# Fewer dense expert blocks, ranked by more heads, and more gathered rows, in a one-core decoder step

## The chip, the cores and the metric

The kernel runs on one core of a Trainium2 chip. The metric is the time of one execution on the device in microseconds. The kernel before took 3285.18 us (median of three runs, 3284.6 to 3286.1).

## The reference, cut to what matters

One layer of a decoder trunk is computed for 512 prompt tokens and 64 sample tokens of width 2048: modulated norm, an input projection, a recurrent and a convolutional head group, an output projection, and then PEER, an expert layer that takes most of the time. Everything is float32.

```python
q = (xb @ w_q).reshape(PEER_BLOCK, PEER_HEADS, 2, HALF_DIM)          # 8 heads
sc = jnp.einsum('thpk,pnk->thpn', q, sub_keys)                       # 2 x 128 keys
v1, i1 = lax.top_k(sc[:, :, 0], 16); v2, i2 = lax.top_k(sc[:, :, 1], 16)
cand = v1[..., :, None] + v2[..., None, :]
cidx = i1[..., :, None] * N_KEYS + i2[..., None, :]
top, pos = lax.top_k(cand, 16)
eidx = jnp.take_along_axis(cidx, pos, axis=-1)                       # 16 of 16384 experts per head
g = jax.nn.softmax(top, axis=-1)
act = jax.nn.gelu(jnp.einsum('td,thkd->thk', xb, expert_u[eidx])) * g
return jnp.einsum('thk,thkd->td', act, expert_v[eidx])
```

A token thus has 8 x 16 = 128 picks among 16,384 experts. The 128 experts that share a first key `i1` are called a block here; there are 128 blocks.

## The kernel before

**Two ways to an expert.** The blocks are ranked by how often the prompt tokens choose their first key. The first `L` = 84 in rank are dense: every prompt token is multiplied with all 128 experts of such a block, and the products count with the gate weight, which is zero where the token did not pick the expert. Picks in the other 44 blocks, and all picks of the sample tokens, are gathered: an indirect DMA fetches one row of `u` or `v` (2,048 floats, 8,192 bytes) for each of 128 partitions, and VectorE multiplies it.

**Dense part.** A block's matrix is split into two float32r parts, `xhi` on ScalarE (line 904) and `xlo` on GpSimd (line 905), and a product takes three matmuls (hi x hi, hi x lo, lo x hi). The u products come first: `u_half` (line 1357) works on half a block at a time, 24 matmuls of 128x512, so 168 half blocks. They then leave `actd` in DRAM. The v products follow in steps of four blocks by a quarter of the width: `v_column` (line 1377) is called four times in a step with 12 matmuls each. `GROUPS` says over how many blocks a PSUM sum runs before VectorE adds it into `acc` (line 1399); the first group's sum is copied by ScalarE. There are M = 84 steps; the last nine are the tail, with the norm and the output beside them, and all gathered rows must be used by the step ahead of them (`last = M - VQ - ENDS`).

**Gate weights.** `g_pair`, `g_scale`, `g_mm` and `g_out` build, for eight tokens at a time, the weights of all dense blocks as a product of two one-hot matrices (line 1555) during the u products, and `g_out` writes them to DRAM, `gd`. For every four blocks (`sg`) `load_group` brings `actd` back as `actr`, `load_weights` brings the weights as `gsb` in four quarters on ScalarE's DMA queue, `weigh` multiplies them on VectorE (line 1320), and `halve` makes the two parts `ahi` (ScalarE) and `alo` (VectorE, line 1331) for the v products. The dictionary `jobs` says at which column of which step each of these is issued.

**Gathered part.** `count` counts each token's picks outside the dense blocks, `sort` orders the tokens by that count, and `SORTED` cuts the order into groups (first token, tokens, slots). A group of 128 tokens has a slot column for each pick; in a group of 64 each token has two partitions ("lanes"), so twice the picks. `slots` finds the picks by repeated top-8 (lines 1168 and 1170). Places without a pick get an index beyond the table, which moves nothing. `gather_u` first loads the group's tokens (`h2r`, then `hT` on ScalarE, line 1218), then fetches a row per slot (line 1203, issued by GpSimd) and takes the dot product (`dot`, line 1231); `gather_v` multiplies and adds into `accB` (line 1259) and at the end scatters the sum to `accd` with an indirect DMA (line 1270), a group's second lane by an accumulating one. The 64 sample slots come first. So there are 64 + 147 = 211 rows of u and as many of v. If a token has more picks than its slots, `flag` is set, and a branch at the end computes all picks of the groups exactly, 128 u and 128 v rows for each.

**Order.** All this is laid out by hand: from the last head's queries on, each engine runs its instructions in the order in which the program issues them. Inside a loop over half blocks, the generator `choice` (last head, softmax, count, sort), then `all_slots`, hand out pieces with a cost, and rows are issued by `RATE` until the slots are done, evenly after that. `EARLY_V` v rows are used during the u products, the rest in the v products, spread evenly over columns; up to four rows are fetched ahead there. `E0` is the half block from which the weights are all written and the first two `sg` are loaded. A block's number is read from `blk` by SyncE when its load is issued.

**Ranking.** `choose` adds, for the first `HEADS_COUNTED` = 4 heads, which keys are in a token's top 8 (`cnt`, line 754). `rank_keys` mixes these counts with a guess from the keys' norms and leaves `perm` and `blk`, before the last heads are computed.

Of the kernel before, what the change touches and what calls it, by code (L numbers as in the profile page):

```python
# [30 lines left out]
NA = NP  # L31
NG = T - NA
NE = 128
L = 84
SG = 4
GROUPS = (8,) * 10 + (4,)
# [5 lines left out]
SORTED = ((0, 64, 34), (64, 128, 43), (192, 128, 33), (320, 128, 27), (448, 64, 10))  # L42
# [6 lines left out]
RATE = (1.0, 1.7)  # L49
PIECE_G = 6.3  # L50
HEADS_COUNTED = 4
FULL_ROWS = 1.25
LAG = 3
PAIRS = 6
EARLY_V = 24
# [24 lines left out]
def build(ctx, tc, A, O, dbg=None):  # L80
# [598 lines left out]
    actp.tile([128, 24], F32, name="shift_l", bufs=1)  # L679
# [19 lines left out]
    gd = dr.tile([NCH, 128, L, TC], F32, name="gd")  # L699
# [46 lines left out]
    def choose(h, s, z):  # L746
# [6 lines left out]
        if h < HEADS_COUNTED and z != "S":  # L753
            V.scalar_tensor_tensor(cnt, s[:, 0:128], 0.5 * NEG, cnt, op0=ALU.is_lt, op1=ALU.add)
# [175 lines left out]

    def rank_keys():

        row = rt2.tile([128, 128], F32, name="rk_row")
        q = rt2.tile([128, 128], F32, name="rk_q")
        low = rt2.tile([128, 128], F32, name="rk_low")
        c = rt2.tile([128, 3], F32, name="rk_c")
# [13 lines left out]
        yield  # L950
        pk = pbank("g", "rk1", 2)
        PE.transpose(pk[:, 0:128], row, ident)
        V.tensor_copy(c[:, 0:1], pk[:, 0:1])
# [6 lines left out]
        PE.matmul(pk[:, 0:128], rowi.to_broadcast([128, 128]), low, start=True, stop=True)  # L960
        V.tensor_copy(perm, pk[:, 0:128])
        V.tensor_copy(blk, perm[0:1, :])
        yield

# [189 lines left out]
    def slots(i):  # L1154
# [19 lines left out]
        if n < 128:  # L1174
            V.tensor_copy(sl[n:, :, 0:c], sl[n:, :, c:2 * c])
# [65 lines left out]
    def gather_v(i):  # L1241
# [7 lines left out]
        def add(j):  # L1249
# [22 lines left out]
            for o in range(0, 128, n):  # L1272
                after.append([gu[0] + 2 + 4 * (o > 0), lambda o=o: out(o)])
# [6 lines left out]
    VO = (0, 2, 1, 3, 5, 4)  # L1280
# [179 lines left out]
    def choice():  # L1460
# [97 lines left out]
    def g_out(b, pg):  # L1558
# [15 lines left out]
    E0 = NU2 - 18  # L1574
# [24 lines left out]
    for n in range(NU2):  # L1599
# [61 lines left out]
        for sg, o, first in ((0, 1, 0), (1, 8, 1)):  # L1661
            if n - E0 == o + 1:
                load_group(sg)
            if 0 <= n - E0 - o + first < 4:
# [232 lines left out]
```

## Time and profile before

| | |
|---|---|
| median of the runs, us | 3285.18 (3284.6 to 3286.1) |
| profiled execution, us | 3270.15 |
| its span, us | 3268.2 |
| mean granted TensorE clock | 0.979 |
| TensorE, VectorE, ScalarE, GpSimd busy in the span | 95%, 66%, 33%, 53% |
| HBM read, written, MB | 865.21, 68.90 |
| first u product, first v product, us | 1198.9, 2263.0 |

The profile is one execution, read from the hardware's records. TensorE's busy time is modelled and its matmuls overlap, so how long a row of them took is read from the chain of work that ended last, where pieces stand with start and length. An engine's row in a table by stretches gives busy time with the number of instructions; "idle before" names what ended the wait. A DMA share of 1 means that the core's 16 DMA engines had packets in work all the time.

### The profile page before, as it was taken

To read this page: it belongs to the slowest core of one execution; us is meant where nothing else is said; L and a number is where in the kernel's file an instruction comes from. 1 tells how busy PE (TensorE), PEld (TensorE's weight loads), DVE (VectorE), ACT (ScalarE), POOL (GpSimd) and SP (SyncE) were. 2 spreads that over 40 slices of the span, in tenths; PEclk is the share of its full clock that TensorE was granted. 3 is DMA by queue.
4 is the path that set the end of the run, shared out by engine and by line. 5 is a ranking of instruction groups with operands and counts; after the bars stand their busy time and mean duration, and the time that the engine had idled before them with its cause. 6 is when DMAs were issued, how large, how long until landed. Compare 5 with 4: busy or idle time off the path is not lost.

```text
span 3268.2 us, 53659 instructions
## 1 busy us (share of the span) xinstructions
PE 3113.4 (95%) x20695; PEld 2636.8 (81%) x20695; DVE 2144.7 (66%) x3238; ACT 1074.2 (33%) x1672; POOL 1725.1 (53%) x985
## 2 busy tenths in 40 slices
PE   5999999999989999999989999998999999999997
PEld 2688889899979998887778888776788877788776
DVE  5455521243346898887988888856667787778745
ACT  3244311132232222222656666522322222222222
POOL 2233233344343336666656666656767676777642
PEclk8999999999989999999999999999999999999998
DMA  9834566624342228989879898999999988898964
GB/s 363 298 136 140 172 214 207 209 82 135 128 156 70 70 89 280 314 315 371 314 287 387 323 391 337 375 353 350 369 354 374 376 310 287 324 366 323 353 189 146
DMA packets 305109, 869.09 MB, mean 266 GB/s; under 512 B 37610, under 2 KB 81514, under 8 KB 256650
## 3 DMA queue, kind: packets, MB, share of 16 engines
q1 hardware_dynamic: 165216, 390.87, 34.6%
q0 software_dynamic: 62880, 386.64, 30.2%
q10 hardware_dynamic: 76752, 88.10, 7.8%
q8 instruction: 163, 2.67, 0.3%
q14 instruction: 98, 0.80, 0.1%
HBM read 865.21 MB, written 68.90 MB: 286 GB/s over the span
## 4 chain that ended last, share of the span: by engine, by line
PE 55%; DMA 6%; issue 4%; DVE 2%; POOL 2%; ACTq 0%; ACT 0%; SPq 0%; POOLq 0%; DVEq 0%
PE pu L1357 23%; PE pv L1377 22%; PE qb L138 3%; PE qa L138 3%; DMA gsb<-gd 2%; DMA raw<-v 1%; POOL xlo L905 1%; PE gbank L1555 1%; PE gx L1555 1%; DMA v<-v,rows 1%; DMA u<-u,rows 1%; PE sc L740 0%; DVE accB L1259 0%; PE pv L1381 0%; DMA tok<-accd 0%
## 5 line engine op out<-in xcount | busy, mean ns | idle before, releaser
L905 POOL TENSOR_TENSOR xlo<-raw,xhi 128x1024 fp32r<-128x1024 f32 x336 | 824.0, 2463 | 506.0 <-ACT xhi L904 502.5
L904 ACT ACTIVATE xhi<-raw 128x1024 fp32r<-128x1024 f32 x336 | 355.0, 1061 | 898.5 <-PE pv L1377 405.2
L1231 DVE SCALAR_TENSOR_TENSOR u<-u,hT 128x2048 f32<-128x2048 f32 x211 | 478.3, 2283 | 152.6 <-DMA u<-u,rows 145.1
L1259 DVE SCALAR_TENSOR_TENSOR accB<-v,dots,accB 128x2048 f32<-128x2048 f32 x199 | 468.2, 2353 | 153.2 <-DMA v<-v,rows 151.3
L1377 PE MATMUL pv<-ahi,xhi 128*128 128x512 f32 x1344 | 530.8, 395 | 16.6 <-DVE acc L1399 9.1
L1377 PE MATMUL pv<-ahi,xlo 128*128 128x512 f32 x1344 | 528.7, 393 | 10.1 <-POOL xlo L905 10.1
L1357 PE MATMUL pu<-hhi,xhi 128*128 128x512 f32 x1344 | 533.4, 397 | 3.2 <-ACT xhi L904 2.6
L1357 PE MATMUL pu<-hhi,xlo 128*128 128x512 f32 x1344 | 525.3, 391 | 7.3 <-POOL xlo L905 7.3
L1377 PE MATMUL pv<-alo,xhi 128*128 128x512 f32 x1344 | 528.2, 393 | 0.0
L1357 PE MATMUL pu<-hlo,xhi 128*128 128x512 f32 x1344 | 525.1, 391 | 0.0
L1377 PEld LDWEIGHTS pv<-ahi,xhi 128*128 128x128 f32 x1344 | 255.4, 190 | 72.2 <-DVE acc L1399 7.7
L1377 PEld LDWEIGHTS pv<-ahi,xlo 128*128 128x128 f32 x1344 | 255.4, 190 | 67.1 <-POOL xlo L905 13.7
L1357 PEld LDWEIGHTS pu<-hhi,xhi 128*128 128x128 f32 x1344 | 253.3, 188 | 63.5 <-ACT xhi L904 3.4
L1357 PEld LDWEIGHTS pu<-hhi,xlo 128*128 128x128 f32 x1344 | 253.3, 188 | 63.2 <-POOL xlo L905 9.5
L1377 PEld LDWEIGHTS pv<-alo,xhi 128*128 128x128 f32 x1344 | 255.4, 190 | 52.7
L1357 PEld LDWEIGHTS pu<-hlo,xhi 128*128 128x128 f32 x1344 | 253.4, 189 | 50.1
L1203 POOL DMA_INDIRECT v<-v,rows x211 | 243.6, 1154 | 89.0 <-issue 33.5
L1203 POOL DMA_INDIRECT u<-u,rows x211 | 213.5, 1012 | 125.4 <-DVE u L1231 75.8
L1549 ACT ACTIVATE op<-op,it 128x128 f32<-128x128 f32 x512 | 155.4, 388 | 1.4 <-issue 0.9
L127 POOL TENSOR_TENSOR wlo_q<-raw_q,whi_q 128x1024 fp32r<-128x1024 f32 x28 | 68.0, 2430 | 151.9 <-ACT whi_q L125 151.9
L188 PE MATMUL ada<-wa,cpad 128*32 128x512 f32 x768 | 106.5, 650 | 42.9 <-DMA wa<-w_ada 42.9
L1399 DVE TENSOR_TENSOR acc<-acc,pv 128x512 f32<-128x512 f32 x144 | 96.2, 682 | 74.7 <-PE pv L1377 74.6
(482 smaller groups left out, 5501.4 us busy)
## 6 DMA issues: line engine op xcount, KB each, us to landing
wa<-w_ada SPq DMA_DIRECT2D x96, 1024.0 KB
raw<-ut SPq DMA_DIRECT2D x168, 512.0 KB
raw<-v SPq DMA_DIRECT2D x336, 256.0 KB
actd<-act ACTq DMA_DIRECT2D x84, 256.0 KB
gd<-stg ACTq DMA_DIRECT2D x64, 336.0 KB
gsb<-gd ACTq DMA_DIRECT2D x84, 256.0 KB
actr<-actd ACTq DMA_DIRECT2D x21, 1024.0 KB
raw_o<-w_out SPq DMA_DIRECT2D x32, 512.0 KB
```

Of the source, the lines that this page charges most:

```text
L127: lo_engine(share).tensor_sub(lo, raw, r32(hi))
L138: PE.matmul(o, st, mv[pick](k), start=first, stop=last)
L188: PE.matmul(acc[32 * g:32 * g + 32, :], cpad[:, 4 * kq + g, :], w[:, g, :], start=kq == 0, stop=kq == 3)
L904: S.activation(hi, raw, AF.Copy)
L905: G.tensor_sub(lo, raw, r32(hi))
L1203: G.indirect_dma_start(out=out, out_offset=None, in_=src, in_offset=bass.IndirectOffsetOnAxis(ap=idx, axis=0), bounds_check=NE * 128 - 1, ...
L1231: V.scalar_tensor_tensor(r, r, 1.0, st["h"], op0=ALU.mult, op1=ALU.mult, accum_out=dots[i][:, j:j + 1])
L1259: V.scalar_tensor_tensor(st["a"], r, dots[i][:, j:j + 1], st["a"], op0=ALU.mult, op1=ALU.add)
L1357: PE.matmul(pu, st[:, kk, :], movA[mv](k), start=k == 0 and a == 0, stop=k == KD - 1 and a == 2)
L1377: PE.matmul(pv, st, mv, start=first and j == 0 and a == 0, stop=last and not end and j == SG - 1 and a == 2)
L1399: V.tensor_add(ak, ak, pv)
L1549: S.activation(ops[:, j0 + j, :], ops[:, j0 + j, :], AF.Copy, scale=it[2][:, b * 4 + j:b * 4 + j + 1])
```

## The change

- `L` is 80 in place of 84, so there are 160 half blocks of u and 80 steps of v. The first v group has 4 blocks, then nine of 8 and one of 4; eleven groups as before.
- The count `cnt` takes all eight heads. After the last head, `rank_again` ranks once more by these counts alone, with the first 24 blocks of the first ranking kept in place (their loads are already under way); its matmuls and VectorE work are issued between the pieces of `choice`.
- Six sorted groups with 152 slots take the place of five with 147: two of 32 tokens in four lanes, one of 64 in two, three of 128. A group in four lanes ends with one plain and three accumulating outputs, four row uses apart.
- `gd` is laid out as [group of four blocks, partition, chunk of tokens, 4 x 32]; the puts write 512-byte runs and the loads of `gsb` read 2,048-byte runs. Before, they were runs of 2,688 and 512 bytes.
- Rows and timing constants: `EARLY_V` 8 in place of 24, `E0` 13 half blocks ahead of the end in place of 18, the first `RATE` 0.85 in place of 1.0, and the splits of the second `sg` move into the first v step.

```diff
-L = 84
+L = 80
-GROUPS = (8,) * 10 + (4,)
+GROUPS = (4,) + (8,) * 9 + (4,)
-SORTED = ((0, 64, 34), (64, 128, 43), (192, 128, 33), (320, 128, 27), (448, 64, 10))
+SORTED = ((0, 32, 20), (32, 64, 25), (96, 128, 42), (224, 128, 33), (352, 128, 27), (480, 32, 5))
-RATE = (1.0, 1.7)
+RATE = (0.85, 1.7)
+FIXED = 24
-EARLY_V = 24
+EARLY_V = 8
...
-    gd = dr.tile([NCH, 128, L, TC], F32, name="gd")
+    gd = dr.tile([L // SG, 128, NCH, SG * TC], F32, name="gd")
...
-        if h < HEADS_COUNTED and z != "S":
+        if z != "S":
             V.scalar_tensor_tensor(cnt, s[:, 0:128], 0.5 * NEG, cnt, op0=ALU.is_lt, op1=ALU.add)
...
+    def rank_again():
+        row, low, c = rk_row, rk_low, rk_c
+        pk = pbank("g", "rk4", 2)
+        PE.matmul(pk[:, 0:128], ones, cnt, start=True, stop=True)
+        PE.matmul(pk[:, 128:256], c[:, 1:2].to_broadcast([128, 128]), ident, start=True, stop=True)
+        V.tensor_scalar(low, iota, rowi, None, op0=ALU.is_lt)
+        yield
+        V.tensor_scalar(row, pk[:, 128:256], -1.0, float(FIXED), op0=ALU.mult, op1=ALU.add)
+        V.tensor_scalar(row, row, 0.0, float(16 * NA), op0=ALU.max, op1=ALU.mult)
+        V.tensor_add(row, row, pk[:, 0:128])
+        yield
+        yield from rank_rows(True)
...
             for o in range(0, 128, n):
-                after.append([gu[0] + 2 + 4 * (o > 0), lambda o=o: out(o)])
+                after.append([gu[0] + 2 + 4 * (o // n), lambda o=o: out(o)])
...
-    VO = (0, 2, 1, 3, 5, 4)
+    VO = (0, 3, 1, 2, 4, 6, 5)
...
         nc.scalar.dma_start(gsb[sg][:, 4 * q:4 * q + 4, :],
-                            gd[4 * q:4 * q + 4, :, sg * SG:(sg + 1) * SG, :].rearrange("c p i t -> p c (i t)"))
+                            gd[sg, :, 4 * q:4 * q + 4, :])
...
+        again = rank_again()
         for z in late:
             for _ in resolve(z, HD - HB):
+                next(again, None)
                 yield 9.5
             yield 5.5
             yield next(picked, 0.0)
+            next(again, None)
...
-            for q in range(0, L, L // 4):
-                puts.append(lambda q=q: nc.scalar.dma_start(gd[c][:, q:q + L // 4, :], full[:, q:q + L // 4, :]))
+            for q in range(0, L // SG, L // SG // 4):
+                puts.append(lambda q=q: nc.scalar.dma_start(
+                    gd[q:q + L // SG // 4, :, c, :].rearrange("g p x -> p g x"),
+                    full[:, SG * q:SG * q + L // 4, :].rearrange("p (g i) t -> p g (i t)", i=SG)))
...
-    E0 = NU2 - 18
+    E0 = NU2 - 13
...
-    hi_at = -4
+    hi_at = 0
+    jobs[0] = [lambda: halve(1, 0)]
+    jobs[2] = [lambda: halve(1, 1)]
```

VectorE late in the v products, in one pass over a quarter of the width, before: `pv` sums are added to `acc` as TensorE finishes them, and between them stand gathered rows (`accB`) and the split `alo`.

```order
L1399 TENSOR_TENSOR acc<-acc,pv_5_26315 128x512
L1331 TENSOR_TENSOR alo_26393<-actr_26131,ahi_26392 128x2048
L1399 TENSOR_TENSOR acc<-acc,pv_6_26335 128x512
L1259 SCALAR_TENSOR_TENSOR accB_25691<-v_21_26328,dots_14532,accB_25691 128x2048
L1399 TENSOR_TENSOR acc<-acc,pv_7_26353 128x512
L1259 SCALAR_TENSOR_TENSOR accB_25691<-v_22_26348,dots_14532,accB_25691 128x2048
L1259 SCALAR_TENSOR_TENSOR accB_25691<-v_23_26409,dots_14532,accB_25691 128x2048
L1259 SCALAR_TENSOR_TENSOR accB_25691<-v_24_26442,dots_14532,accB_25691 128x2048
L1399 TENSOR_TENSOR acc<-acc,pv_8_26492 128x512
```

The same place now:

```order
L1424 TENSOR_TENSOR acc<-acc,pv_5_26598 128x512
L1284 SCALAR_TENSOR_TENSOR accB_26240<-v_15_26611,dots_16030,accB_26240 128x2048
L1424 TENSOR_TENSOR acc<-acc,pv_6_26617 128x512
L1356 TENSOR_TENSOR alo_26695<-actr_26426,ahi_26694 128x2048
L1424 TENSOR_TENSOR acc<-acc,pv_7_26637 128x512
L1284 SCALAR_TENSOR_TENSOR accB_26240<-v_16_26630,dots_16030,accB_26240 128x2048
L1284 SCALAR_TENSOR_TENSOR accB_26240<-v_17_26689,dots_16030,accB_26240 128x2048
L1284 SCALAR_TENSOR_TENSOR accB_26240<-v_18_26711,dots_16030,accB_26240 128x2048
L1284 SCALAR_TENSOR_TENSOR accB_26240<-v_19_26770,dots_16030,accB_26240 128x2048
L1284 SCALAR_TENSOR_TENSOR accB_26240<-v_20_26788,dots_16030,accB_26240 128x2048
L1424 TENSOR_TENSOR acc<-acc,pv_8_26775 128x512
```

Between the sums `pv_5` and `pv_8` stand six rows in place of four.

GpSimd in the v products, from the first to the second output of the group whose tokens have the most picks, before (`accd` is the output, `v` a row fetch, `xlo` a split for TensorE):

```order
L1270 DMA accd<-v_33_26766,tok 512x2048
L905 TENSOR_TENSOR xlo_26935<-raw_26748,xhi_26934 128x1024
L905 TENSOR_TENSOR xlo_26939<-raw_26757,xhi_26938 128x1024
L1203 DMA v_4_26960<-v,rows_8663 128x2048
L1203 DMA v_5_26991<-v,rows_8663 128x2048
L1203 DMA v_6_27009<-v,rows_8663 128x2048
L905 TENSOR_TENSOR xlo_27028<-raw_26842,xhi_27027 128x1024
L905 TENSOR_TENSOR xlo_27032<-raw_26851,xhi_27031 128x1024
L1203 DMA v_7_27067<-v,rows_8663 128x2048
L1270 DMA accd<-v_33_26766,tok 512x2048
L1203 DMA v_8_27086<-v,rows_8663 128x2048
```

The same group's second and third of four outputs now:

```order
L1295 DMA accd<-v_19_26122,tok 512x2048
L1228 DMA v_8_26402<-v,rows_8660 128x2048
L1228 DMA v_9_26421<-v,rows_8660 128x2048
L1228 DMA v_10_26441<-v,rows_8660 128x2048
L905 TENSOR_TENSOR xlo_26460<-raw_26266,xhi_26459 128x1024
L905 TENSOR_TENSOR xlo_26464<-raw_26275,xhi_26463 128x1024
L1228 DMA v_11_26498<-v,rows_8660 128x2048
L1295 DMA accd<-v_19_26122,tok 512x2048
L1228 DMA v_12_26530<-v,rows_8660 128x2048
```

Where the group's sum left in two outputs, it leaves in four, with four row fetches and two splits between them, and the row's buffer is held until the last.

More of the change, by code (lines that the diff above doesn't have):

```diff
@@ L678, in build @@
     actp = ctx.enter_context(tc.tile_pool(name="actp", bufs=3))
-    actp.tile([128, 24], F32, name="shift_l", bufs=1)
     gp = ctx.enter_context(tc.tile_pool(name="gp", bufs=1))
@@ L929, in query_out @@
         qs.setdefault(h, []).append(q)
+    rk_row = rt2.tile([128, 128], F32, name="rk_row")
+    rk_q = rt2.tile([128, 128], F32, name="rk_q")
+    rk_low = rt2.tile([128, 128], F32, name="rk_low")
+    rk_c = rt2.tile([128, 3], F32, name="rk_c")
     def rank_keys():
[L933 to L936, printed above, removed]
+        row, q, low, c = rk_row, rk_q, rk_low, rk_c
         V.tensor_scalar(low, iota, rowi, None, op0=ALU.is_lt)
@@ L950, in rank_keys, with rank_rows @@
         yield
+        yield from rank_rows()
+    def rank_rows(apart=False):
+        row, q, low, c = rk_row, rk_q, rk_low, rk_c
         pk = pbank("g", "rk1", 2)
         PE.transpose(pk[:, 0:128], row, ident)
+        if apart:
+            yield
         V.tensor_copy(c[:, 0:1], pk[:, 0:1])
@@ L960, in rank_keys @@
         PE.matmul(pk[:, 0:128], rowi.to_broadcast([128, 128]), low, start=True, stop=True)
+        if apart:
+            yield
         V.tensor_copy(perm, pk[:, 0:128])
@@ L963, in rank_keys @@
         yield
+    def rank_again():
[4 more added lines that the diff above has]
+        V.tensor_scalar(low, iota, rowi, None, op0=ALU.is_lt)
+        yield
+        V.tensor_scalar(row, pk[:, 128:256], -1.0, float(FIXED), op0=ALU.mult, op1=ALU.add)
+        V.tensor_scalar(row, row, 0.0, float(16 * NA), op0=ALU.max, op1=ALU.mult)
+        V.tensor_add(row, row, pk[:, 0:128])
+        yield
+        yield from rank_rows(True)
     ranking = rank_keys()
@@ L1173, in slots @@
         V.tensor_copy(thr[:, i:i + 1], sl[:, 0, m - 1:m])
-        if n < 128:
-            V.tensor_copy(sl[n:, :, 0:c], sl[n:, :, c:2 * c])
+        for r in range(n, 128, n):
+            V.tensor_copy(sl[r:r + n, :, 0:c], sl[r:r + n, :, r // n * c:(r // n + 1) * c])
         us = pools["rs"].tile([128, c], F32, name=f"us{i}", tag="us", bufs=1)
@@ L1660, in build @@
         u_half(n, i, c)
-        for sg, o, first in ((0, 1, 0), (1, 8, 1)):
+        for sg, o in ((0, 1), (1, 7)):
             if n - E0 == o + 1:
                 load_group(sg)
-            if 0 <= n - E0 - o + first < 4:
-                load_weights(sg, n - E0 - o + first)
-            if n - E0 == o + 5 + sg:
+            if 0 <= n - E0 - o < 4:
+                load_weights(sg, n - E0 - o)
+            if n - E0 == o + 5:
                 weigh(sg)
-            if n - E0 == o + 6 + sg:
+            if n - E0 == o + 6:
                 halve(sg, 0)
-            if n - E0 == o + 7 + sg:
+            if n - E0 == o + 7:
                 halve(sg, 1)
@@ L1784, in build @@
             V.tensor_mul(w, w, R_[:, 1, :])
-            if n < 128:
-                V.memset(w[n:], 0.0)
+            for r in range(n, 128, n):
+                V.memset(w[r:r + n], 0.0)
             V.tensor_scalar(kk[:, 0, :], R_[:, 0, :], -1.0, 0.0, op0=ALU.add, op1=ALU.max)
```

## The prediction

> **What bounds the kernel now.** I read the page first, then the stretches by time, the chain that ended last, the groups by line and the waits. The execution falls into four pieces: before the dense blocks (to 1198.9 us), the dense u products (to 2263.0, the first `pv` matmul), the dense v products up to the step by which every gathered row must be used (to 3114.0), and the tail.
>
> The page's first part, then those stretches (columns: length, busy time of each engine with instructions, granted clock, share of the DMA engines, GB/s), with three windows inside the v stage:
>
> ```profile
> PE 3113.4 (95%) x20695; PEld 2636.8 (81%) x20695; DVE 2144.7 (66%) x3238; ACT 1074.2 (33%) x1672; POOL 1725.1 (53%) x985
> ```
>
> ```profile
> 1100.00:1200.00 100.00, 99.34 (x724) 97.26 (x724) 98.84 (x424) 23.94 (x42) 32.05 (x14) 0.98 0.22 75
> 1198.90:2263.00 1064.10, 1035.41 (x8229) 840.48 (x8229) 861.08 (x1255) 491.01 (x936) 657.03 (x420) 0.99 0.88 333
> 2263.00:3114.00 851.00, 830.54 (x3601) 682.00 (x3602) 636.73 (x365) 202.56 (x193) 605.59 (x348) 0.98 0.93 340
> 3114.00:3268.20 154.20, 124.80 (x613) 104.74 (x611) 74.42 (x92) 33.77 (x43) 47.72 (x22) 0.89 0.51 171
> 2300.00:2400.00 100.00, 100.00 (x443) 82.77 (x442) 68.57 (x32) 31.35 (x34) 75.10 (x41) 1.00 1.00 366
> 2400.00:2500.00 100.00, 100.00 (x443) 82.81 (x442) 71.15 (x44) 22.86 (x21) 65.39 (x38) 1.00 0.97 354
> 2500.00:2600.00 100.00, 100.00 (x443) 82.81 (x442) 80.14 (x48) 23.79 (x21) 75.07 (x44) 1.00 1.04 399
> ```
>
> TensorE hardly rests, so it is the bound. But from 2300 to 2600 the DMA engines are full too (share 1.00, 0.97, 1.04 at 366, 354, 399 GB/s) and TensorE still loses nothing: the two limits lie close together, and the change pushes them in opposite directions. The chain shows what a matmul really costs:
>
> ```profile
> 1248.92 212.18 PE pu L1357 x936
> ...
> 2296.50 245.46 PE pv L1377 x1082
> ```
>
> 212.18/936 = 0.2267 us and 245.46/1082 = 0.2269 us; the 391 to 397 ns that the groups give as a mean overlap. The groups that the sum needs, and the busy time of the gate-weight matmuls (L1555) within the u stage:
>
> ```profile
> L1231 DVE SCALAR_TENSOR_TENSOR u<-u,hT 128x2048 f32<-128x2048 f32 x211 | 478.3, 2283 | 152.6 <-DMA u<-u,rows 145.1
> L1259 DVE SCALAR_TENSOR_TENSOR accB<-v,dots,accB 128x2048 f32<-128x2048 f32 x199 | 468.2, 2353 | 153.2 <-DMA v<-v,rows 151.3
> ...
> L1203 POOL DMA_INDIRECT v<-v,rows x211 | 243.6, 1154 | 89.0 <-issue 33.5
> ```
>
> ```profile
> 1198.90:2263.00 1064.10, 90.36 (x4096) 76.96 (x4096) 0.99 0.88 333
> ```
>
> The u stage then holds 84 x 48 = 4032 block matmuls (914.1 us), 90.4 us of gate matmuls, and 1064.1 - 914.1 - 90.4 = 59.6 us of holdups. The v stage holds 75 steps of 48 (816.6 us) and 34.4 us of holdups.
>
> **The change part by part.** *Four blocks fewer.* In the u stage 4 x 48 matmuls go: 192 x 0.2267 = 43.5 us. The gate matmuls are 80 columns wide in place of 84: 90.4 x 4/84 = 4.3 us. In the v stage there are 71 steps ahead of the last ones in place of 75: 192 x 0.2269 = 43.6 us. All of it is TensorE's own time, so all of it is on the path if nothing else takes its place. The tail keeps its nine steps; I take it as unchanged (bounds -5 to +5).
>
> *More rows to gather.* What dense blocks do not cover is fetched as rows of 8,192 bytes. I counted the picks outside the dense blocks from the reference's inputs with each kernel's ranking rule: 14,627 before, 15,908 after; unused places of a slot move nothing. The queue's row of the page bears the first count out:
>
> ```profile
> q0 software_dynamic: 62880, 386.64, 30.2%
> ```
>
> 14,627 x 2 x 8,192 bytes are 239.6 MB, the 64 sample slots 134.2 MB, tokens, picks and outputs 12.7 MB: 386.5 MB. The changed kernel also takes only 8 v rows ahead of the v stage in place of 24, so that stage now gathers 216 - 8 = 208 rows where it had 211 - 24 = 187. The v stage's traffic was:
>
> ```profile
> DMA packets 122538, 289.68 MB, mean 340 GB/s; under 512 B 13773, under 2 KB 52685, under 8 KB 101965
> ## 3 DMA queue, kind: packets, MB, share of 16 engines
> q0 software_dynamic: 27824, 168.09, 50.1%
> q1 hardware_dynamic: 44352, 80.76, 27.7%
> q10 hardware_dynamic: 50304, 40.11, 14.9%
> ```
>
> Added: 16 sample rows (16.8 MB), 1,281 picks (10.5 MB), one more group's output (1.0 MB). Removed: four steps of v (4.2 MB) and one set of weights and activations (2.1 MB). That makes 289.7 + 22.0 = 311.7 MB, while TensorE's floor falls to 71 x 48 x 0.2269 = 773 us. To keep that floor the DMA engines would have to move 403 GB/s throughout; at 399, the best window above, they need 781 us. So in the v stage the transfers become the bound. What rate they hold is the main unknown: the stage's own mean of 340 gives 917 us, the best window 781. I go by the three windows above, where the queues were full all along: their mean is 373.
>
> *Weights stored by four blocks.* The reads of `gd` become runs of 2,048 bytes in place of 512. Queue q1, almost all 2,048-byte runs here, took 0.277 x 16 x 851 us / 80.76 MB = 46.7 us per MB; q10, about half of it these short runs, 0.149 x 16 x 851 / 40.11 = 50.6. If its other half costs 46.7, the short runs cost 54.5, and 18.9 MB x 7.8 / 16 = 9 us of DMA time goes, 1.1% of the stage. The rate becomes 377 and the stage 311.7/0.377 = 827 us: 24 us less than 851, not 43.6. The writes of `gd` in the u stage become the short runs instead (20 MB; by the same rows some 10 us of DMA time, in a stage whose DMA share is 0.88): taken at nothing, 10 us if that room is gone.
>
> *VectorE in the v stage.* 636.7 + 21 rows x 2.353 - 6 = 680 us, 82% of 827: dense, not the bound. GpSimd has 21 x 1.154 us more and eight splits fewer (about 20 us): level.
>
> *Holdups of the u stage.* Three things add to the 59.6 us. First who waited for the first ranking's count, then the reloads of `hT`.
>
> ```profile
> PE rk L947: 4.8, 1
> ```
>
> ```profile
> L1218 ACT ACTIVATE hT<-h2r x5: 1861/1882/1883, 1571.8 to 2123.6; 128x2048 f32<-128x2048 f32 x5
> its engine sat idle before it (us, times) until:
>   DMA u<-u,rows: 145.1, 80
>   DMA h2r<-h2d,tok: 11.4, 2
>   DVE u L1231: 8.2, 3
> ```
>
> The second ranking puts three TensorE matmul groups behind VectorE; the old ranking's one such wait was 4.8 us, and all u matmuls queue behind it: 0 to 15, taken 3, since each now stands a step behind its inputs. A sixth group is one more reload of `hT`, for which ScalarE waited 11.4 + 8.2 = 19.6 us over five, with the splits queued behind: 0 to 12, taken 3. By the order of GpSimd's instructions the last 20 half blocks of the u stage issue 37 rows where they had 29: eight more at up to 1.05 MB, 8.4 MB or 21 us at 399 GB/s, of which some fits the slack: 0 to 21, taken 8. The sorting's eight more rounds hide beside matmuls:
>
> ```profile
> L1168 DVE MAX8 sl<-kk 128x8 f32<-128x128 f32 x81 | 22.1, 284 | 0.0
> L1170 DVE MATCH_REPLACE8 kk<-sl,kk 128x128 f32<-128x128 f32 x66 | 18.2, 276 | 0.0
> ```
>
> They are 8 x 3 x 0.56 = 13 us of a VectorE that is busy 861 of 1064 us; without that cover they cost 13.
>
> *Counting all heads* adds 12 operations ahead of the dense blocks, 0.27 us each at the median,
>
> ```profile
> L754 DVE SCALAR_TENSOR_TENSOR cnt<-s,cnt x16: 259/274/1335, 996.1 to 1098.0; 128x128 f32<-128x128 f32 x16
> ```
>
> on an engine that was 98.8% busy there: 3 us, bounds 0 and 6.
>
> *Outputs in four parts.* After an accumulating output GpSimd stood still, with the splits for TensorE queued behind:
>
> ```profile
> 2835.29 1.49 POOL L1270 DMA_INDIRECT accd<-v,tok  x1 [0.30 <-issue]
> 2845.68 1.03 POOL L1203 DMA_INDIRECT v<-v,rows  x1 [8.90 <-DMA accd<-v,tok]
> ```
>
> Accumulating outputs rise from 2 to 7, in three groups in place of two; the next fetch takes the buffer only after a group's last part, so I count one more holdup, 4 us, inside the 827; at most 45 if every one of five more waited 8.9.
>
> **The sum.** u stage -43.5 - 4.3 + 14 = -34; v stage -24; ahead of them +3: -55 us. The profiled execution took 3270.15 us around its span of 3268.2, so 3215; the three runs' median is 3285.18, 15 us above it, and I carry that offset: 3230.
>
> **A rule against the change.** The windows moved 399 GB/s for 100 us with TensorE at work. The Trainium skill, page "DMA: Bandwidth & Descriptors", section "Specifications", gives an HBM limit of about 358 GB/s for a core. By it the v stage would take 871 us and the sum would be +20 - 34 + 3 = -11. The trace disagrees: 399 and 366 stand in windows that are almost all reads. It stays as a small rival.
>
> **The rivals.**
> *The transfers have more room (0.22).* If the wide weight reads end the late arrivals that held ScalarE,
>
> ```profile
> ACT xhi L904 <- DMA gsb<-gd: 23.0, 2, 14.5
> ```
>
> the v stage keeps 399 GB/s: 781 plus 10 of start-up, -60; with no new holdups in the u stage -48; +1 ahead: 3178. For it: 399 held with 512-byte reads under way. Against it: only one window of three reached it. The same skill page, section "Queues, rings and completion order", says that an engine takes turns between queues packet by packet; by that, wider packets get the weights a larger share when all is full, which speaks for this rival; no row here separates it.
>
> *VectorE sets the pace (0.12).* In the dense stretch 13 rows stand between two weight products where 11 stood; with a late row nothing is made up. 16 columns of TensorE last 43.6 us, and if each of 17 such spaces ran 2 us long: 34 us lost, 21 us saved in all: 3264.
>
> *Slower (0.09).* The transfers keep the mean that the stage reached before: 340 GB/s, v stage 917 us, +66 - 34 + 3 = +35: 3320. It decides at 311.7 MB / (851 + 31) us = 353 GB/s. For it: row reads and block reads stall each other through buffers, and the stage held 340 although queues were often full. Against it: its lulls were times when little was asked for.
>
> *The ceiling of 358 (0.05):* 3274.
>
> *The change doesn't do what it says (0.02).* If one token had more picks than its group's slots (by my count 41 of 42 in the third, 48 of 50 in the second, 32 of 33), the exact path at the end would run: 6 x 256 rows at 2.3 us or more, over 3.5 ms.
>
> **How the numbers follow.** Forecast 3230 with 0.50, by itself 3208 to 3252 from the bounds of the u holdups and of a rate 370 to 390. The range 3185 to 3275 takes in VectorE's case, the ceiling and about half of the faster case; left out are the other half (0.10) and the slower ones (0.11). A difference below 0.2% (6.6 us) is not told from none: faster 0.86 (forecast, the faster rival, VectorE's case, a little of the ceiling), same 0.05, slower 0.09.
>
> **What would show it.** Right: the u stage near 1030 us; the v stage (71 steps) near 827 at about 377 GB/s and a DMA share near 1; 15,908 picks on queue q0 (about 410 MB in all). Wrong: v stage waits of `acc` or `accB` that end on VectorE work, not on DMA; a u stage above 1050, with TensorE waiting for the second ranking; a v stage above 880.

## The result, and the profile after

The changed kernel takes 3316.29 us (median of four runs, 3311.51 to 3328.07); the kernel before took 3284.89 beside it (3280.25 to 3286.1). The ratio is 1.0113, with a 95% interval of 1.0086 to 1.014: 1.1% slower (the quotient of the two medians, 1.0096, lies inside the interval). The forecast was 3230, with a range up to 3275, so the sign was wrong. The profiled execution took 3320.15 us, its span is 3318.4 and its mean granted clock 0.965.

The page's first part, then the three stretches (length, busy time of each engine with instructions, granted clock, DMA share, GB/s) of the changed kernel:

```profile
PE 3073.4 (93%) x20330; PEld 2586.5 (78%) x20330; DVE 2215.7 (67%) x3377; ACT 1050.0 (32%) x1653; POOL 1707.2 (51%) x987
```

```profile
1207.10:2290.90 1083.80, 1019.95 (x8056) 818.50 (x8057) 879.01 (x1399) 475.89 (x924) 631.54 (x402) 0.97 0.85 313
2290.90:3165.50 874.60, 801.66 (x3410) 649.86 (x3409) 685.89 (x387) 192.88 (x185) 611.09 (x368) 0.97 0.95 360
3165.50:3318.40 152.90, 124.20 (x613) 104.72 (x611) 77.66 (x93) 33.87 (x43) 48.80 (x22) 0.89 0.54 172
```

The work for TensorE did shrink: 3840 block matmuls for u and as many for v, in place of 4032. But the u stage, forecast at 1030 us, takes 1084, and the v stage, forecast at 827, takes 875; before they took 1064 and 851. Taking block and gate matmuls off as the prediction did (3840 x 0.2267 + 86 = 957 us; 71 x 48 x 0.2269 = 773), the holdups come to 127 us in the u stage, where they were 60, and 101 in the v stage, where they were 34. Not all of a holdup is standing: TensorE's busy time leaves 64 us idle in the u stage (1083.80 - 1019.95; 29 before) and 73 in the v stage (20 before). Half or more of the rest are matmuls that start further apart than 0.227 us, as shown below. The stretch ahead of the blocks is 8 us longer in these two profiles; over all profiles below it ends at 1198 to 1207 us with four heads counted (mean 1202) and at 1201 to 1209 with eight (mean 1206). That is about the 3 us that were forecast, though the two ranges overlap. The count of rows was right: queue q0 was to carry about 410 MB.

```profile
q0 software_dynamic: 64736, 409.85, 31.4%
```

**Where the u stage lost it.** The chain of waits in the changed kernel from 1640 to 1668 us (start, length, what), a stretch with one of its longest stops:

```profile
by line: ACTq L1595 39.3%; PE pu L1382 25.0%; ACT op L1577 8.6%; ACTq L904 6.7%; PE gx L1583 6.6%; ACT stg L1590 4.9%; ACT xhi L904 3.8%; PE gbank L1583 2.9%; ACT act L1385 1.7%; issue 0.9%
...
1644.46 1.22 ACTq L1595
...
1645.71 9.78 ACTq L1595
...
1659.83 5.16 PE pu L1382 x12
```

and the same place on ScalarE's and TensorE's rows of the timeline (start, length, instruction, and in brackets the idle time before it):

```profile
1643.40 1.06 ACT L904 ACTIVATE xhi<-raw 128x1024 fp32r<-128x1024 f32 x1 [1.91 <-issue]
1643.42 12.07 ACTq L1595 DMA_DIRECT2D gd<-stg  x2
1655.54 2.46 ACT L1577 ACTIVATE op<-op,it 128x128 f32<-128x128 f32 x8 [11.07 <-issue]
...
1655.99 1.38 PE L1583 MATMUL gbank<-wr,op 128*32 128x80 f32 x32 [4.30 <-ACT op L1577]
1658.53 1.30 PE L1583 MATMUL gx<-wr,op 128*32 128x80 f32 x32 [1.16 <-ACT act L1385]
...
1660.78 0.63 PE L1382 MATMUL pu<-hhi,xlo 128*128 128x512 f32 x1
1661.20 0.63 PE L1382 MATMUL pu<-hhi,xhi 128*128 128x512 f32 x1
```

Line 1595 is the put of `gd`. ScalarE does not wait for data here: it stands 12 us inside the instructions that issue two puts. The activations behind them (`op`, for the gate matmuls, and `act`) come late, and TensorE's queue stops at the gate matmuls, for 4.3 and 1.2 us. It then runs slower for a while: the granted clock from 1659.8 to 1665.0 us is 0.55, the matmuls start 0.43 us apart, and the next 12 take 5.16 us in the chain, where 12 x 0.2267 would be 2.7. So this stop of 12 us on ScalarE cost TensorE some 8 us, a third of it by the clock. Over the whole u stage, steps of more than 0.3 us between neighbouring block matmuls add 31 us to the idle time, 13 before. With rows_nothing, below, there are few stops and the granted clock of both stages is 1.00, so the lower clock goes with the stops. The put's line, with nanoseconds as least / median / most, first in the changed kernel, then in the one before:

```profile
L1595 ACTq DMA_DIRECT2D gd<-stg x64: 366/632/9778, 1602.5 to 2184.8; - x64
```

```profile
L1567 ACTq DMA_DIRECT2D gd<-stg x64: 326/446/2371, 1600.9 to 2149.1; - x64
```

Added up from the trace, the 64 issues take 81 us in place of 34. The groups by stage show that the bytes are not it: q10 used 12.7% of the 16 engines' time in the u stage, 11.6% with the old store (rows under gd_old below).

**Where the v stage lost it.** The same view in eight stretches of the changed kernel's v stage, and three of before's:

```profile
2290.90:2400.00 109.10, 99.86 (x416) 81.51 (x415) 77.91 (x38) 33.25 (x38) 74.07 (x44) 0.94 1.00 386
2400.00:2510.00 110.00, 110.00 (x487) 91.09 (x486) 90.12 (x53) 24.92 (x22) 80.75 (x45) 1.00 1.01 388
2510.00:2620.00 110.00, 105.42 (x454) 85.41 (x453) 87.03 (x50) 25.52 (x23) 77.22 (x49) 0.98 0.99 381
2620.00:2730.00 110.00, 102.49 (x440) 83.18 (x440) 90.98 (x54) 23.79 (x22) 78.23 (x49) 0.98 0.96 364
2730.00:2840.00 110.00, 101.56 (x433) 81.42 (x433) 85.91 (x52) 21.63 (x20) 81.78 (x50) 0.98 0.92 346
2840.00:2950.00 110.00, 93.17 (x389) 75.31 (x388) 84.11 (x47) 21.65 (x20) 70.35 (x44) 0.92 0.93 341
2950.00:3060.00 110.00, 100.57 (x436) 80.88 (x436) 90.15 (x55) 24.42 (x23) 78.78 (x48) 1.00 0.91 348
3060.00:3165.50 105.50, 88.58 (x366) 71.05 (x365) 79.67 (x45) 17.71 (x17) 69.91 (x45) 0.94 0.87 326
```

```profile
2476.00:2582.00 106.00, 106.00 (x469) 87.77 (x468) 85.80 (x52) 26.79 (x24) 79.34 (x47) 1.00 1.03 391
2582.00:2688.00 106.00, 101.88 (x448) 83.73 (x447) 81.46 (x49) 22.71 (x21) 76.37 (x46) 1.00 0.87 314
2688.00:2794.00 106.00, 102.82 (x445) 84.16 (x445) 82.87 (x48) 23.39 (x21) 72.49 (x43) 0.98 0.80 284
```

For 329 us the transfers move 381 to 388 GB/s with a share of 1; then the rate falls to 326 to 364 at a share of 0.87 to 0.96, while TensorE loses more than before. The three windows on which I built the v stage's rate (2300 to 2600) all lay in the first 40% of the stage. Who waits, in the changed kernel's v stage (us in total, times, longest):

```profile
...
ACT xhi L904 <- DMA raw<-v: 233.9, 48, 15.7
DVE accB L1284 <- DMA v<-v,rows: 158.0, 111, 7.4
...
POOL v L1228 <- DMA accd<-v,tok: 40.9, 4, 14.2
...
PE pv L1402 <- DVE acc L1424: 37.4, 23, 4.2
...
PE pv L1402 <- POOL xlo L905: 27.0, 7, 8.0
```

Before, the same waits were

```profile
...
DVE accB L1259 <- DMA v<-v,rows: 129.6, 60, 8.2
ACT xhi L904 <- DMA raw<-v: 93.4, 26, 8.8
...
POOL v L1203 <- DMA accd<-v,tok: 13.7, 3, 8.9
...
PE pv L1377 <- POOL xlo L905: 10.1, 6, 5.4
...
PE pv L1377 <- DVE acc L1399: 9.1, 4, 3.0
```

TensorE waits for VectorE's `acc` and GpSimd's `xlo`. VectorE itself stands waiting for rows (158 us) and is busy for 686 of 875 us, and the split `xlo` needs ScalarE's `xhi`, which waits for blocks (234 us): all three feeding engines wait for transfers more than before. That transfers are the cause is shown by rows_nothing below.

### The profile page after: what moved, and what is told of

The parts are those of the page before. It is cut to its first block, busy times and chain, and to the rows that moved or that the text cites. A ratio compares the mean times of both kernels' runs of the same rounds, so it can differ in the third digit from the quotient of the medians.

```text
span 3318.4 us, 52898 instructions
## 1 busy us (share of the span) xinstructions
PE 3073.4 (93%) x20330; PEld 2586.5 (78%) x20330; DVE 2215.7 (67%) x3377; ACT 1050.0 (32%) x1653; POOL 1707.2 (51%) x987
## 4 chain that ended last, share of the span: by engine, by line
PE 43%; DMA 11%; issue 5%; DVE 4%; POOL 3%; ACTq 1%; ACT 1%; SPq 0%; POOLq 0%; DVEq 0%
PE pu L1382 21%; PE pv L1402 12%; DMA raw<-v 5%; DMA v<-v,rows 4%; PE qb L139 3%; PE qa L139 2%; POOL xlo L905 2%; PE gx L1583 1%; PE gbank L1583 1%; ACTq L1595 1%; DVE accB L1284 1%; POOL v L1228 1%; DVE u L1256 1%; POOL u L1228 1%; DMA gsb<-gd 1%
## 5 line engine op out<-in xcount | busy, mean ns | idle before, releaser
L905 POOL TENSOR_TENSOR xlo<-raw,xhi 128x1024 fp32r<-128x1024 f32 x320 | 782.6, 2455 | 485.5 <-ACT xhi L904 480.4
L904 ACT ACTIVATE xhi<-raw 128x1024 fp32r<-128x1024 f32 x320 | 338.2, 1062 | 942.0 <-PE pv L1402 319.1
L1256 DVE SCALAR_TENSOR_TENSOR u<-u,hT 128x2048 f32<-128x2048 f32 x216 | 489.9, 2284 | 173.5 <-DMA u<-u,rows 171.1
L1402 PE MATMUL pv<-ahi,xhi 128*128 128x512 f32 x1280 | 511.5, 400 | 46.0 <-DVE acc L1424 37.4
L1382 PE MATMUL pu<-hhi,xhi 128*128 128x512 f32 x1280 | 516.9, 404 | 16.9 <-ACT xhi L904 11.1
L1402 PE MATMUL pv<-ahi,xlo 128*128 128x512 f32 x1280 | 507.4, 396 | 27.0 <-POOL xlo L905 27.0
L1382 PE MATMUL pu<-hhi,xlo 128*128 128x512 f32 x1280 | 507.5, 396 | 13.6 <-POOL xlo L905 13.6
L1382 PE MATMUL pu<-hlo,xhi 128*128 128x512 f32 x1280 | 507.1, 396 | 0.0
L1402 PE MATMUL pv<-alo,xhi 128*128 128x512 f32 x1280 | 506.0, 395 | 0.0
L1228 POOL DMA_INDIRECT v<-v,rows x216 | 246.6, 1142 | 133.4 <-DMA accd<-v,tok 40.9
L1382 PEld LDWEIGHTS pu<-hhi,xhi 128*128 128x128 f32 x1280 | 246.0, 192 | 77.6 <-ACT xhi L904 12.4
L128 POOL TENSOR_TENSOR wlo_o<-raw_o,whi_o 128x1024 fp32r<-128x1024 f32 x32 | 77.8, 2431 | 115.8 <-ACT whi_o L126 106.2
```

The source lines that it names most:

```text
L128: lo_engine(share).tensor_sub(lo, raw, r32(hi))
L904: S.activation(hi, raw, AF.Copy)
L905: G.tensor_sub(lo, raw, r32(hi))
L1228: G.indirect_dma_start(out=out, out_offset=None, in_=src, in_offset=bass.IndirectOffsetOnAxis(ap=idx, axis=0), bounds_check=NE * 128 - 1, ...
L1256: V.scalar_tensor_tensor(r, r, 1.0, st["h"], op0=ALU.mult, op1=ALU.mult, accum_out=dots[i][:, j:j + 1])
L1382: PE.matmul(pu, st[:, kk, :], movA[mv](k), start=k == 0 and a == 0, stop=k == KD - 1 and a == 2)
```

## The experiments

Each run stood beside runs of the kernel before on the same chip; ratios are to those. Stage lengths come from one profiled execution of each kernel and repeat to some 10 us: the v stage, which `put_one`, `puts_sync` and `after_mended` leave as it is, took 864.8, 874.0 and 863.4 us. Against the median of its runs the profiled execution of before lies 15 us low, that of gd_old 21 high, of rank_once 14 high, of blocks_only 11 high and of six_once 11 low; where two of these are compared, the medians decide and the stages only say roughly where.

### What the rows cost, and the parts one by one

**rows_nothing**: fetches are issued but every index lies beyond the table, so no row moves; the dot products are multiplied with zero. This leaves the gathered picks out of the result.

```diff
-bounds_check=NE * 128 - 1, oob_is_err=False
+bounds_check=127, oob_is_err=False
...
-    V.scalar_tensor_tensor(r, r, 1.0, st["h"], ...)
+    V.scalar_tensor_tensor(r, r, 0.0, st["h"], ...)
```

> The changed kernel with every row fetch still issued, but with indices above 127 out of bounds, so that almost no bytes of gathered rows move (the dot products are multiplied by zero; the gathered picks are left out of the output). Theory T, transfers: the added holdups of both stages come from rows and blocks that arrive late because the DMA engines are full. Then the u stage falls from 1084 us to 980 to 1010, the v stage from 875 to 785 to 810, and the time to about 3316 - 160 = 3155. Rival O, order: the holdups come from the instructions themselves, VectorE and GpSimd in program order with 13 rows between two weight products. Then both stages stay within 30 us of what they are and the time stays above 3260.

3149.69 us, ratio 0.9609 [0.9592, 0.9626]. Its two stages:

```profile
1207.60:2207.20 999.60, 988.21 (x8055) 801.61 (x8056) 875.90 (x1400) 476.78 (x924) 631.53 (x403) 1.00 0.45 139
2207.20:2993.60 786.40, 776.84 (x3409) 640.83 (x3408) 686.15 (x386) 193.46 (x184) 624.44 (x367) 1.00 0.56 154
```

VectorE and GpSimd do the same work as in the changed kernel, yet the holdups are only 43 and 13 us, as theory T had it. So the order of the instructions is not what holds it; the traffic is. The puts, too, are quick when the queues are empty:

```profile
L1595 ACTq DMA_DIRECT2D gd<-stg x64: 366/481/1328, 1583.5 to 2127.0; - x64
```

**rank_once**: `if h < HEADS_COUNTED and z != "S":` as before, and no `next(again, None)`. The rest is the change.

> The changed kernel with the first ranking alone, counted by four heads as before (80 blocks, six groups and all else as changed; 16,261 picks are gathered in place of 15,908). Theory R, the second ranking holds TensorE: the 9.1 us of holdup in half blocks 15 and 16 go, and 4 to 8 us ahead of the first block, so 3316 - 15 = 3301. Theory T: the 353 picks more are 5.8 MB, 15 us at 390 GB/s, and take that back: 3312 to 3325.

3320.87, ratio 1.0116 [1.0091, 1.0142]: no different from the whole change, inside theory T's range. The second ranking's own wait is there,

```profile
PE rk L959 <- DVE rk_row L986: 6.2, 1, 6.2
```

(in the changed kernel). It costs more than this wait: worked out as the holdups above, the first 20 half blocks hold TensorE up for 16 us in the changed kernel and 6 in rank_once. Over all profiles that fetch rows it is 15 to 17 with two rankings and 6 to 8 with one. Without it 5.8 MB more move in the two stages, and later half blocks lose the time again.

**gd_old**: the change with the old store of the weights.

```diff
-    gd = dr.tile([L // SG, 128, NCH, SG * TC], F32, name="gd")
+    gd = dr.tile([NCH, 128, L, TC], F32, name="gd")
...
-                            gd[sg, :, 4 * q:4 * q + 4, :])
+                            gd[4 * q:4 * q + 4, :, sg * SG:(sg + 1) * SG, :].rearrange("c p i t -> p c (i t)"))
...
-            for q in range(0, L // SG, L // SG // 4):
...
+            for q in range(0, L, L // 4):
+                puts.append(lambda q=q: nc.scalar.dma_start(gd[c][:, q:q + L // 4, :], full[:, q:q + L // 4, :]))
```

> The changed kernel with the weights stored as before (written in runs of 2,560 bytes, read in runs of 512). If the wide reads help the v stage and the short writes cost the u stage nothing, it is 9 to 25 us slower than the changed kernel: 3325 to 3340. Rival: the short writes hold ScalarE's queue in the u stage (5 to 25 us) and it is as fast or faster: 3290 to 3316.

3281.51, ratio 1.001 [0.9991, 1.0029]: below both expectations, so the new store alone costs 1.0%, 35 us. Its stages, the put, and queue q10 in its u stage, then in the changed kernel's:

```profile
1209.00:2252.90 1043.90, 1004.79 (x8055) 809.94 (x8056) 874.48 (x1398) 476.63 (x924) 630.71 (x401) 0.98 0.87 325
2252.90:3146.30 893.40, 813.11 (x3409) 655.51 (x3409) 677.83 (x389) 191.88 (x184) 608.32 (x368) 0.96 0.96 353
```

```profile
L1595 ACTq DMA_DIRECT2D gd<-stg x64: 326/444/1234, 1602.8 to 2150.0; - x64
```

```profile
q10 hardware_dynamic: 25872, 45.88, 11.6%
```

```profile
q10 hardware_dynamic: 55568, 45.88, 12.7%
```

40 us less in the u stage, 19 more in the v stage, where the reads are narrow again; as this profile lies 21 us high, the 19 may be little or nothing in a typical run.

**blocks_only**: gd_old and rank_once together, with five groups: 80 blocks and the change's step constants, nothing else. Beyond those two edits:

```diff
-SORTED = ((0, 32, 20), (32, 64, 25), (96, 128, 42), (224, 128, 33), (352, 128, 27), (480, 32, 5))
+SORTED = ((0, 64, 34), (64, 128, 46), (192, 128, 35), (320, 128, 29), (448, 64, 11))
...
-    VO = (0, 3, 1, 2, 4, 6, 5)
+    VO = (0, 2, 1, 3, 5, 4)
```

> 80 blocks with the changed kernel's step constants, but one ranking, the old store of the weights and five groups (34, 46, 35, 29 and 11 slots, 155 in all, 16,261 picks). Theory T: the trade of four blocks for rows is itself what loses; with 5.8 MB more rows it is no faster than the changed kernel: 3310 to 3335. Rival P, the parts beside it lose (second ranking, short writes, outputs in four parts): 3240 to 3285.

3269.84, ratio 0.9973 [0.9959, 0.9987]: the blocks alone gain 0.3%, 9 us, not the 48 + 44 us that their matmuls last. Rival P has it. Its u stage took 1045.9 us, its v stage 873.1. Of its 89 us of holdups in the u stage, 30 lie in the last 20 half blocks, where before lost 18 and rows_nothing loses 7.

**five_twice** (gd_old with five groups of 39, 45, 35, 28 and 10 slots, two rankings) and **six_once** (gd_old with rank_once's edit):

> Old store, second ranking, but five groups (39, 45, 35, 28 and 10 slots of 64, 128, 128, 128, 64 tokens). If the six groups cost the 12 us between the runs with the old store (3281.5) and with the blocks alone (3269.8) and the ranking pays its 6 to 9 us of waiting back with its 4 MB fewer rows: 3265 to 3273 us. If the ranking costs it: 3279 to 3286 us.

> Old store, one ranking, six groups. If the groups cost the 12 us: 3279 to 3290 us. If the ranking does: 3266 to 3273 us. If it is the difference of two noisy medians, both runs of this call lie within 5 us of each other.

3287.58, ratio 1.0039 [1.0023, 1.0055], and 3277.22, ratio 1.0019 [1.0002, 1.0037]. Against blocks_only, the second ranking alone costs 0.7% and the six groups alone 0.5%; both together (gd_old) cost 0.4%. None of them gains anything, though the ranking saves 5.8 MB of rows. five_twice lies 2 us above the range for "the ranking costs it" and six_once between its two ranges; since the parts don't add up, what each costs by itself stays open.

**early24**: the change with `EARLY_V = 24`.

> After, with 24 instead of 8 of the v steps fetched during the u stage, as before has it. 16 steps of 1.05 MB move from the v stage to the u stage. If each stage is held up by its bytes at its own rate (313 and 360 GB/s): u plus 54, v minus 47, 3318 to 3328 us. If the u stage has room that these steps can use (its halves 17 to 47 and 100 to 140 hold up little in after), u rises by less than 35 and the v stage gives 40 to 47: 3295 to 3312 us. If what holds up the v stage is ScalarE's and GpSimd's own queues and not bytes, v gains less than 20 and the time rises to 3330 or more.

3333.99, ratio 1.015 [1.0116, 1.0184]. The u stage took 1126.9 us (+43), the v stage 853.9 (-21): the rows moved cost more where they went than where they came from. 32 of the 43 us lie in the last 20 half blocks (68 us of holdups in place of 36). The time, 3330 or more, is the one that the theory of the queues gave, but its v gain was to be under 20; the theory of the bytes gave 54 and 47 and at most 3328. In the v stage the run doesn't separate the two.

### The store of the weights

**before_gd_new**: the kernel before with the new layout, puts of 5, 5, 5 and 6 groups of blocks on ScalarE.

```diff
-                puts.append(lambda q=q: nc.scalar.dma_start(gd[c][:, q:q + L // 4, :], full[:, q:q + L // 4, :]))
+                puts.append(lambda q=q, e=e: nc.scalar.dma_start(
+                    gd[q:e, :, c, :].rearrange("g p x -> p g x"),
+                    full[:, SG * q:SG * e, :].rearrange("p (g i) t -> p g (i t)", i=SG)))
```

> Before, with only the new store of the weights (84 blocks: runs of 512 bytes written, of 2048 read; puts of 5, 5, 5 and 6 groups by ScalarE). If the store costs by itself what old and new store differ by in after (35 us): 3295 to 3320 us; the page's own prices were plus 35 to 40 us in the u stage and minus 19 in the v stage, which gives 3290 to 3300. If it costs only where the rows are crowded into the end of the u stage, as in after, the u stage stays at 1064 and the v stage gains 15 to 20: 3258 to 3268 us.

3290.47, ratio 1.0041 [1.0022, 1.006]. The u stage took 1092.4 us (+28), the v stage 843.7 (-7). The store costs by itself, with 84 blocks too, and less than beside 80. Yet its 64 issues took 89 us in all, more than the 81 in the changed kernel: how much of an issue's length reaches TensorE depends on what stands around it.

**puts_sync**: one word, `nc.scalar.dma_start` to `nc.sync.dma_start`, in the put of the changed kernel.

> After, with one edit: the 64 puts of gd are issued by SyncE instead of ScalarE; layout, bytes and 512-byte runs are those of after. Theory A (the queue): what costs is the time ScalarE spends issuing. In the trace of after the 64 puts take 81 us of ScalarE's queue, the longest 9.8, against 32 us with the old layout, and while it stands the gate's activations, and TensorE behind them, wait. With the puts on SyncE the u stage's time beyond its matmuls falls from 127 us to 80 to 95, the v stage stays near 874: 3270 to 3290 us, below the run with the old layout. Theory B (the memory): 40,960 writes of 512 bytes take that much more of the transfers wherever they are issued: 3308 to 3325 us. Rival C (the blockage moves): SyncE, which issues the weights of TensorE's next blocks behind the puts, stands instead, and u's weights come late: 3300 us or more, with waits of xhi on raw<-ut that after does not have.

3292.04, ratio 1.0035 [1.0016, 1.0054]: 24 us of the 35 come back with the same runs and bytes, so most of the price goes with the issue on ScalarE; theory B falls. But so does the plain form of theory A: the time lies 2 us above its range, and the u stage's holdups come to 111 us, not to 80 to 95. The load of u's blocks, queued behind the puts on SyncE, and who waits for it:

```profile
L888 SPq DMA_DIRECT2D raw<-ut x160: 332/333/17382, 1185.2 to 2231.5; - x160
```

```profile
ACT xhi L904 <- DMA raw<-ut: 116.7, 26, 12.7
```

In the changed kernel:

```profile
ACT xhi L904 <- DMA raw<-ut: 13.9, 3, 7.6
```

SyncE's 160 load issues grew from 53 to 171 us in all, the longest 17.4 us, while ScalarE's `actd` issues, up to 14 us in the changed kernel, never took more than 0.34. The stop belongs to the queue that carries the short runs, and hits whatever is issued next on it. This is rival C, in part.

**put_one**: the changed kernel with `put(1)` for `put(2)` in each half block.

> After, with one edit: at most one put of gd per half block instead of two; layout, runs, bytes and ScalarE's queue are those of after. Theory A (the queue fills): a put of 640 short runs goes fast while the queue is empty (0.48 us in the run that fetches nothing) and is held while the one ahead of it is still under way (in after two puts of one half block took 12.1 us at 1643). With a half block of some 6.6 us between two puts the sum of the 64 issues falls from 81 us to below 60 and the time to 3285 to 3305 us. Theory B (the memory): the same short runs take the same time from the transfers, 3308 to 3325 us.

3300.29, ratio 1.0057 [1.0045, 1.007]. Theory A's two numbers are met (3285 to 3305; 64 issues in 36 us). But only 16 of the 35 us come back, and the u stage's profile still has 123 us of holdups. So the length of the issues is not the whole price. One of ScalarE's waits in that stage:

```profile
ACT stg L1590 <- DMA gd<-stg: 27.6, 3, 15.1
```

`stg` has two buffers; the next chunk's eviction waits until an earlier chunk's put has landed. From the issue of a put to its last packet, by the trace's packet records, passed at the median 8.3 us with the old store (gd_old), 12.5 in the changed kernel, 12.4 here and 3.1 in rows_nothing. In the changed kernel this wait is 5.6 us, in gd_old there is none; a third buffer was not tried.

**five_sync** (blocks_only with the new store and its puts on SyncE), **five_sync_one** (and one put per half block) and **five_act_one** (the same with the puts on ScalarE):

> 80 blocks, one ranking, five groups, as in the run of the blocks alone, but with the new store of the weights and its puts issued by SyncE. Theory A: that run's 3270 less the v stage's gain from reading wide (19 us by the profiles of old and new store): 3245 to 3262 us, faster than both kernels. Theory B: the short writes keep their price of 35 to 40 in the u stage: 3280 to 3295 us.

> Five groups, one ranking, new store, puts by SyncE as in the last call's fastest run (3262), one put per half block instead of two. Theory A: SyncE's issues of gd<-stg and raw<-ut, 91 and 143 us there, fall towards 32 and 53, and the u stage's time beyond its matmuls from 93 to 75 to 88 us: 3245 to 3260 us. Theory B: no change, 3256 to 3268 us.

> The same with the puts on ScalarE. Theory A: ScalarE stands for part of what it stands in after, 3255 to 3280 us, above the run on SyncE. Theory B: equal to it within 5 us.

3262.2, ratio 0.9943 [0.9921, 0.9964]; 3247.45, ratio 0.9902 [0.9888, 0.9916]; and 3266.7, ratio 0.9944 [0.9924, 0.9965]. The first lies 0.2 us above the range of theory A, the others inside theirs. In five_sync_one the issues fell to 44 and 88 us, and the u stage's holdups to 70. It beats both kernels, the one before by 1.0%. Its stages:

```profile
1205.80:2232.30 1026.50, 1001.80 (x8037) 802.36 (x8038) 855.64 (x1257) 473.83 (x923) 632.57 (x405) 0.99 0.89 334
2232.30:3083.40 851.10, 809.27 (x3409) 644.32 (x3408) 664.67 (x386) 192.55 (x183) 606.24 (x363) 0.98 0.96 369
```

All three v stages (851.5, 851.1 and 851.7 us) are 22 us shorter than blocks_only's, whose profile lies 11 us high. The wide reads bring some of that; the other pairs give 7 us (before and before_gd_new), 1 (six_once and rank_once) and 19 (gd_old and the changed kernel). In five_act_one evictions wait for puts to land again:

```profile
ACT stg L1588 <- DMA gd<-stg: 42.2, 4, 16.1
```

There is no such wait in five_sync_one. The puts land about as late there (median 12.3 us to 10.9, longest 22.3 to 27.1); why ScalarE's evictions meet them in the one and not in the other isn't settled.

**after_mended**: puts_sync and put_one together.

> After with its puts issued by SyncE, one per half block instead of two. By the run with five groups and one ranking this mend takes 15 us from the run with two puts a half block (3262 to 3247), so 3292 less 12 to 16: 3274 to 3282 us, no faster than before; the ranking and the groups then keep the 30 us that the fastest run lacks them. If the mend is worth more here, since more rows are crowded behind the slots' end: 3255 to 3270 us.

3282.59, ratio 1.0019 [1.0001, 1.0036], half a microsecond above the first range: with its store mended (0.9 of its 1.0% come back) the whole change is no faster than the kernel before. Its u stage takes 1057.7 us, five_sync_one's 1026.5.

## Why the prediction was wrong, step by step

By the ratios the change is blocks (-0.3%, -9 us), groups and ranking (+0.4%, +12 us) and store (+1.0%, +34 us): +37 where -55 was forecast. Sorted in the same way, the forecast had -55 for the blocks with the step constants, +9 for the six groups, the second ranking and the counting, and -9 for the store. So two steps failed by like amounts, the blocks by 46 us and the store by 43. With the old store the change comes out no faster (gd_old, ratio 1.001), with the new one it is slower.

- **The puts of `gd`, "taken at nothing, 10 us if that room is gone".** The DMA time was about right: q10's rows give (12.7% of 1083.8 - 11.6% of 1043.9) = 17 us, beside the 10 of the estimate, spread over the stage. But I priced the transfer and not what it does to the engine that issues it. In the u stage the store cost 40 us (28 in before_gd_new's profile against before's, 62 in rank_once's against six_once's). Of the 1.0% net, by the ratios 0.8 come back by issuing the puts elsewhere (puts_sync), 0.6 by spreading them out (put_one), 0.9 by both (after_mended). That ScalarE's stops are the cause is shown; how they divide into standing in the issue and waiting for a put to land is not. The trace of before held the hint. One of its long puts took 2.4 us to issue where the median was 0.45, and ScalarE's loads of `gsb`, which were already in 512 runs of 512 bytes, took up to 13.5:

```profile
L1314 ACTq DMA_DIRECT2D gsb<-gd x84: 366/367/13536, 2166.0 to 3082.7; - x84
```

- **The wide reads, "1.1% of the stage".** Right in sign; the size stays open. The four pairs of profiles give 1 to 22 us for the 9 that were forecast. One gain had not been foreseen: the issues of `gsb` fell from 57 us in all (gd_old) to 33.
- **The v stage at 377 GB/s.** Here the mechanism was right (the transfers bound it) and the size off. The bytes came to 314.9 MB, not 311.7 (8 us); the rate to 360. blocks_only, with narrow reads, moved 314.7 MB in 873 us, where 373 GB/s would have given 844. The rate was taken from three windows in the first 40% of the stage and laid over all of it; the later windows of before, at 284 and 314 GB/s, I took for lulls "when little was asked for". In the changed kernel, with more to move, they are there again. Why the rate falls there stays open.
- **The u stage's holdups, +14.** In blocks_only they rose by 30, without a second ranking, a sixth group or the new store: of 48 us of matmuls that went, 18 were gained, by profiles that lie 26 us apart against their medians. The rows crowded into the end, "taken 8", are the largest part that can be placed: 12 us more in the last 20 half blocks. The second ranking, taken 3, cost some 9 in the first 20, within the bounds of 0 to 15. The u stage did pass the 1050 us that were named as a sign, but TensorE waited only 6.2 us for the ranking itself. That holdups go with the rows' traffic is shown by rows_nothing; the step constants were not separated, except that `EARLY_V` back at 24 lost 0.4% more (early24).
- **Outputs in four parts, 4 us.** GpSimd's waits behind outputs rose from 13.7 to 40.9 us, but they are 36.4 in blocks_only, which has no such group; no run shows a price for the four parts.
- **The rivals.** The slower rival gave 3320, close to the time that came, but by luck: it needed the v stage below 353 GB/s and a gain in the u stage, and the rate was 360 and the u stage lost. VectorE was not the pace (it waited for rows). The ceiling of 358 GB/s that the Trainium skill states (page "DMA: Bandwidth & Descriptors", section "Specifications") would have given a v stage of 871 us, an estimate with the forecast's bytes, and 874.6 came. Yet it isn't that limit: the same stage held 381 to 388 for 329 us, and five_sync_one 369 over the whole of it.

Two passages of the Trainium skill bear on the step that failed at the store. Its page "Perfetto Trace Analysis", section "DMA Instruction — HWDGE (DVE, Sync)", says that the profiled entry of such a DMA runs from the wait for the descriptor generator through its work to the sequencer's semaphore, and leaves out the movement of the data. The traces agree that the movement is not in it: with idle queues the entry of a put is 0.48 us at the median and its last packet ends 3.1 us after the issue; which part of the entry grew to 9.8 us under load no run here shows. The Trainium skill's page "DMA: Bandwidth & Descriptors", section "Issuing engines are not separate DMA queues", says that another issuing engine saves only issue time, usually small beside the transfer; here moving the issue was worth 24 us.

## What to carry to other kernels

A DMA has a price on the engine that issues it, and here it grew with the number of its runs once the queues were busy: before splitting a store into short runs to make a load wide, look at what stands behind the put on its engine, move it to the queue that has least to lose, and spread the puts out. When work is moved from an engine to the transfers, take the transfers' rate from the whole stage or its worst part, not from the windows where they were at their best. A short stop of TensorE can cost more than its length, since the matmuls behind it may run at a lower clock. Undo each part by itself: here one part of the change (the blocks) gained, one (the store) was worth having in another form, and two (the ranking and the groups) brought no gain.

## What the runs showed of the hardware

- The issue of one 320 KB put in 640 runs of 512 bytes took 0.48 us (median) with few rows moving (rows_nothing) and up to 9.8 us under load (12.4 in rank_once); in 128 runs of 2,560 bytes at most 1.9 us under such a load (six_once).
- The stop follows the queue: with the puts on SyncE (puts_sync) its 512 KB loads took up to 17.4 us to issue, in place of 0.36 at most, and ScalarE's stores 0.34 in place of up to 14.
- A 512-byte packet took 27 ns of a DMA engine (changed kernel), a 2,560-byte one 102 (gd_old): for equal bytes a third more, while issue (81 us to 32) and landing (12.5 us to 8.3) differ by more.
- After a stop of TensorE (4.3 us, 1.4 us of work, 1.2 us) its granted clock was 0.55 for some 5 us, and block matmuls started 0.43 us apart in place of 0.227.
